# VectorE's program in source order, a 64-column chunk loop and the first projection ahead of the second, in a hybrid RWKV-7 and Conformer step

## The chip, the cores and the metric

The kernel runs on one core of one Trainium2 chip. The metric is device microseconds of one execution. The engines are TensorE (PE in the profile, its weight loads PEld), VectorE (DVE), ScalarE (ACT), GpSimd (POOL), and SyncE (SP), which issues most DMAs.

## The reference, cut to what matters

One layer for 512 prompt tokens and 8 single-token samples, all in float32; the kernel lays them side by side as 520 columns.

```
xn = _rmsnorm(x, norm_g);  proj = xn @ w_in              # 2048 -> 11392
r, k, v, xw, xa = xs[...]                                # token-shifted columns of proj
decay = exp(-exp(w_log(xw)));  a = sigmoid(a0 + xa @ a_lora_b)
for t:                                                   # per head, S is 64 x 64
    sa = S @ a_t;  S = S * w_t + sa b_t^T + v_t k_t^T;  o_t = S @ r_t
o   = groupnorm(o) + bonus
y_a = (o * silu(gate_a)) @ w_proj_a                      # the first projection
u   = glu(proj);  c = depthwise_conv31(u) + conv_b
y_b = (silu(layernorm(c)) * silu(gate_b)) @ w_proj_b     # the second projection
m   = sigmoid(ga) * y_a + sigmoid(gb) * y_b
h   = x + m @ w_out
h   = h + sigmoid(h @ w_ple_gate) * (p @ w_ple)
y   = _rmsnorm(h) * final_g
```

## The kernel before

Activations lie channel-major, 128 channels by 520 tokens a tile. Every large product goes through `gemm` and `step` (L153 to L175): a step is one 128 x 128 weight tile times 520 columns. Activation and weight are each split in a high part (`wh`, `xh`, `hi`) and a low part (`wl`, `xl`, `lo`), and three of the four products are summed, in two column halves of 260, so a step is six matmuls; there are 2224 steps. `prepare` (L117) makes `wh` on ScalarE and `wl` on VectorE for four steps at a time (a half of a loaded block). It runs two halves ahead of use (`AHEAD`) in four buffers (`WB`). Weights arrive in 512 KB DMAs on SyncE's queue.

The first 16 k-steps make four output tiles at once. Then a loop over eight pairs of heads p runs nine gemms of 16 steps each: k, r, v, gate_a, the two halves of the GLU input, gate_b and two merge gates (`merge`, L652, which stores its sigmoid to DRAM, `sga_d` and `sgb_d`). 16 more merge gates follow, then the two projections (L846), `w_out` (L856), and the gated embedding with the final norm (`gate`, `finish`).

All small work is written as generators that `tick` advances after each step; `yield n` means n steps later. So the numbers behind `yield` set where PE's small matmuls stand between the steps, since PE's order is that of the source (`manual_schedule`, L54). The order on VectorE, ScalarE, GpSimd and SyncE is left to the tile framework's scheduler.

The generators:
- `wkv(p)` (L358): the recurrence of two heads in eight chunks of 64 tokens. It makes decays and keys, the 128 x 128 products within chunks (L446), a triangular inverse in 31 dependent pairs of VectorE instructions (`tm`, `ti`, L480), and then the **chunk loop** (L546). Each turn has three links, `ly` steps apart: `x = ar @ suv` for both heads (L549, with `oc` of the chunk before at L551); `x = ttb @ xs` (L556), whose copy to `suv` is made by VectorE for one head (L557) and ScalarE for the other (L558), with a GpSimd copy `xu` (L561); and the state update `bkt @ suv` (L564), after which VectorE makes the next chunk's `suv` (L568) and the state `sf` (L571). A group norm follows, and 16 64 x 64 transposes (L595, L596).
- `conv(i)` (L621): the depthwise convolution, 30 dependent VectorE instructions `c` (L643).
- `samples` and `lnorm` (L678, L715): the recurrence of the eight samples, and the layer norm of the convolution.
- `finish(h)` (L904): the final norm of token half h, which scales the 16 tiles `h2` by `rf` on VectorE or GpSimd (`ON_POOL`) and stores them in `GROUPS`.

Of the kernel before, what the change touches and what calls it, by code (L numbers as in the profile page):

```python
# [17 lines left out]
P = 128  # L18
# [12 lines left out]
WB, AHEAD, LAST, WARM = 4, 2, 12, 14  # L31
# [6 lines left out]
GROUPS = ([range(4 * _g, 4 * _g + 4) for _g in range(4)],  # L38
          [range(0, 1), range(12, 13), range(1, 4), range(4, 8), range(13, 16), range(8, 12)])
ON_POOL = ((1, 2, 3, 5, 6, 7, 9, 10, 11, 13, 14, 15), (12, 13, 14, 15))  # L40
# [8 lines left out]
TILES += [M_SA + _i for _i in range(16, 32)]  # L49


def body(nc, tc, a):
    with ExitStack() as es:
# [21 lines left out]
        vec, act, gps = nc.vector, nc.scalar.activation, nc.gpsimd  # L75
# [14 lines left out]
        for j in range(KD):  # L90
            seq += [a["wpa"][j], a["wpb"][j]]
# [42 lines left out]

        stream = prepares()
# [115 lines left out]
        def colsum(lhsT, hi, lo, n):  # L251
# [3 lines left out]
            for h in range(0, n, step):  # L255
                o = aux()
                nc.tensor.matmul(o[:, :step], lhsT=lhsT, rhs=hi[:, h:h + step], start=True, stop=False)
                nc.tensor.matmul(o[:, :step], lhsT=lhsT, rhs=lo[:, h:h + step], start=False, stop=True)
# [34 lines left out]
        for i, n, o in ((0, 252, first[3][0]), (252, 252, first[3][1]), (504, 16, first[2][0])):  # L293
            o = o[:, HF:HF + n]
            nc.tensor.matmul(o, lhsT=sums[:, 2, :], rhs=sqs[0][:, i:i + n], start=True, stop=True)
# [3 lines left out]
        sxs.close()  # L299

# [7 lines left out]
        def parts(x, n=T):  # L308
            hi = gp.tile([P, T], F32R, name="hi", tag="g")[:, :n]
            lo = gp.tile([P, T], F32R, name="lo", tag="g")[:, :n]  # L310
            split(x, hi, lo)
# [15 lines left out]
        def shifted(m, o, out):  # L327
# [6 lines left out]
            vec.scalar_tensor_tensor(out, p, omu[:, m:m + 1], q, op0=ALU.mult, op1=ALU.add)  # L334
# [6 lines left out]

        tw = et("tw")
        shifted(M_L, o_lora, tw)
        act(tw[0:64, :], tw[0:64, :], AF.Tanh)
        for i, x in enumerate(parts(tw)):
            for j in range(2):
                act(tw2[half(i), j, :], x[half(j), :].bitcast(F32), AF.Copy)
# [8 lines left out]
        flag = {"inv": None, "done": -1, "loop": -1, "conv": 0, "yp": None}  # L356

        def wkv(p, k, box):  # L358
# [3 lines left out]
            dma(out=lor, in_=a["lora"][:, :, p * P:(p + 1) * P])  # L362
            kk = gt("kk")
# [3 lines left out]
            sh, sl_ = parts(sq)  # L367

            yield 16 if p == 0 else 5
            lorh = kq.tile([P, 2, P], F32R, name="lorh")  # L370
            lorl = kq.tile([P, 2, P], F32R, name="lorl")
            split(lor, lorh, lorl)
            yield 7
            sg = gt("sig")
            av = gt("a")
            for j, (out, off) in enumerate(((sg, O_W0), (av, O_A0))):
                for h in range(2):
                    hs = slice(h * HF, (h + 1) * HF)
                    o = aux()
                    nc.tensor.matmul(o[:, :HF], lhsT=lorh[:, j, :], rhs=tw2[:, j, hs], start=True, stop=False)  # L380
                    nc.tensor.matmul(o[:, :HF], lhsT=lorl[:, j, :], rhs=tw2[:, j, hs], start=False, stop=True)
                    act(out[:, hs], o[:, :HF], AF.Sigmoid, bias=col(off, p))
                yield 2
# [3 lines left out]
            yield 2  # L387
# [33 lines left out]
            yield 8  # L421
# [6 lines left out]
            for h in range(2):  # L428
                s = half(h)
                tt(vec, ar[h][s, :, h, :], ch(kk)[s], ep[s, :, 0:64], ALU.mult)  # L430
                tt(gps, ar[h][s, :, 1 - h, :], ch(r)[s], ep[s, :, 1:65], ALU.mult)
                tt(vec, bk[s, :, h, :], ch(b)[s], ch(em)[s], ALU.mult)
# [4 lines left out]
            yield 9  # L437
# [4 lines left out]
            for c0 in (0, 4):  # L442
                os = [aux().rearrange("p (c x) -> p c x", x=P) for _ in range(2)]
                for c in range(4):
                    for h in range(2):
                        nc.tensor.matmul(os[h][:, c, :], lhsT=bk[half(h), c0 + c].rearrange("p a t -> p (a t)"),  # L446
                                         rhs=ar[h][half(h), c0 + c].rearrange("p a t -> p (a t)"), start=True, stop=True)
                for h in range(2):
# [4 lines left out]
                    tt(vec, nbr[s, c0:c0 + 4, i:i + 64], o[s, :, i:i + 64], mk(s, 64, 64), ALU.mult)  # L453
                    tt(vec, f2(ar[h][u, c0:c0 + 4]), o[u], mk(u, 64 * h, P), ALU.mult)
                    yield 2
# [8 lines left out]
            nc.tensor.transpose(o[:48, :P], sp.rearrange("p a b -> p (a b)"), ident)  # L464
# [10 lines left out]
            yield 5  # L475
# [3 lines left out]
            yield 5  # L479
# [521 lines left out]
```

## Time and profile before

| what | value |
|---|---|
| time, median of 3 runs | 1880.88 us (1878.25 to 1882.21) |
| time of the profiled execution | 1881.83 us |
| its span, first to last instruction | 1880.0 us |
| VectorE, the weights' low parts `wl` (L78) | 386.8 us, 541 times |
| VectorE, the convolution `c` (L643) | 188.9 us, 240 times |
| VectorE, `tm` and `ti` of the inverse | 106.5 us and 72.8 us |
| GpSimd, the copies `xu` (L561) | 51.4 us, 128 times |

A row of the costliest groups or of the windows gives busy time and count of instructions. Matmuls overlap, so what a matmul costs is read from the start of one to the start of the next, in the timeline; its own duration is longer. A timeline row merges equal neighbours: start, length, engine, line, what is written from what, the count, and idle time before it with what ended it. A row of the waits gives who waited for whom: total us, number of waits, the longest. PEclk is the granted TensorE clock as a share of full speed.

### The profile page before, as it was taken

To read this page: it belongs to the slowest core of one execution; us is meant where nothing else is said; L and a number is where in the kernel's file an instruction comes from. 1 tells how busy PE (TensorE), PEld (TensorE's weight loads), DVE (VectorE), ACT (ScalarE), POOL (GpSimd) and SP (SyncE) were. 2 spreads that over 40 slices of the span, in tenths; PEclk is the share of its full clock that TensorE was granted. 3 is DMA by queue.
4 is the path that set the end of the run, shared out by engine and by line. 5 is a ranking of instruction groups with operands and counts; after the bars stand their busy time and mean duration, and the time that the engine had idled before them with its cause. 6 is when DMAs were issued, how large, how long until landed. Compare 5 with 4: busy or idle time off the path is not lost.

```text
span 1880.0 us, 37810 instructions
## 1 busy us (share of the span) xinstructions
PE 1823.0 (97%) x15352; PEld 1782.9 (95%) x15352; DVE 1276.0 (68%) x2337; ACT 771.7 (41%) x1478; POOL 397.7 (21%) x514
## 2 busy tenths in 40 slices
PE   9999999999999999999999999999999999999995
PEld 8998998999999999999999999999999999999995
DVE  6679897697797877977977885495433333334457
ACT  6734335336345354363363332464222222243343
POOL 1212214123213213222231372030111000011103
PEclk9999998999999999999999999999999999999998
DMA  7242332432332323323323343456444433252232
GB/s 229 81 117 72 103 100 69 94 106 81 101 102 83 99 88 98 101 86 88 112 76 94 124 153 120 146 165 201 136 136 136 136 118 96 90 192 95 95 103 91
DMA packets 116367, 211.97 MB, mean 113 GB/s; under 512 B 47312, under 2 KB 55632, under 8 KB 116192
## 3 DMA queue, kind: packets, MB, share of 16 engines
q1 hardware_dynamic: 114592, 207.95, 35.9%
q8 instruction: 120, 1.97, 0.4%
q10 hardware_dynamic: 1600, 1.60, 0.3%
q14 instruction: 55, 0.45, 0.1%
HBM read 184.43 MB, written 25.08 MB: 111 GB/s over the span
## 4 chain that ended last, share of the span: by engine, by line
PE 69%; DVE 19%; issue 4%; ACT 3%; POOL 3%; DMA 1%; SPq 0%; DVEq 0%; POOLq 0%; ACTq 0%
PE mm L165 62%; DVE tm L78 5%; DVE wl L78 4%; DVE ti L484 3%; DVE c L643 2%; PE aux L596 1%; PE aux L165 1%; PE aux L446 1%; PE aux L549 1%; ACT wh L81 1%; DVE p L78 1%; PE aux L595 1%; POOL ar L78 1%; PE aux L564 1%; DVE sq L394 1%
## 5 line engine op out<-in xcount | busy, mean ns | idle before, releaser
L165 PE MATMUL mm<-xh,wh 128*128 128x260 f32 x2784 | 593.3, 295 | 0.9 <-ACT xh L219 0.5
L81 ACT ACTIVATE wh<-w 128x512 fp32r<-128x512 f32 (+1 forms) x541 | 338.5, 627 | 621.0 <-PE mm L165 532.2
L78 DVE TENSOR_TENSOR wl<-w,wh 128x512 fp32r<-128x512 f32 (+1 forms) x541 | 386.8, 717 | 280.3 <-ACT wh L81 276.5
L165 PE MATMUL mm<-xh,wl 128*128 128x260 f32 x2784 | 569.4, 286 | 4.8 <-DVE wl L78 4.8
L165 PE MATMUL mm<-xl,wh 128*128 128x260 f32 x2784 | 568.9, 286 | 0.3 <-DVE xl L220 0.3
L165 PEld LDWEIGHTS mm<-xh,wh 128*128 128x128 f32 x2784 | 437.0, 193 | 9.4 <-ACT wh L81 1.1
L165 PEld LDWEIGHTS mm<-xh,wl 128*128 128x128 f32 x2784 | 436.5, 192 | 5.5 <-DVE wl L78 5.4
L165 PEld LDWEIGHTS mm<-xl,wh 128*128 128x128 f32 x2784 | 437.2, 192 | 0.6 <-DVE xl L220 0.5
L165 PE MATMUL mm<-hi,wl 128*128 128x260 f32 x1600 | 333.4, 283 | 3.1 <-DVE wl L78 3.1
L165 PE MATMUL mm<-hi,wh 128*128 128x260 f32 x1600 | 333.3, 283 | 0.0
L165 PE MATMUL mm<-lo,wh 128*128 128x260 f32 x1600 | 332.6, 283 | 0.0
L165 PEld LDWEIGHTS mm<-hi,wl 128*128 128x128 f32 x1600 | 251.0, 189 | 3.3 <-DVE wl L78 3.3
L165 PEld LDWEIGHTS mm<-hi,wh 128*128 128x128 f32 x1600 | 252.1, 189 | 0.1
L165 PEld LDWEIGHTS mm<-lo,wh 128*128 128x128 f32 x1600 | 251.9, 189 | 0.0
L643 DVE SCALAR_TENSOR_TENSOR c<-u,prm,c 128x482 f32<-128x482 f32 (+14 forms) x240 | 188.9, 787 | 3.8
L561 POOL COPY xu<-suv 64x64 f32<-64x64 f32 x128 | 51.4, 402 | 280.8 <-DVE suv L557 271.6
L78 DVE TENSOR_TENSOR tm<-ti,ni 128x16 f32<-128x16 f32 (+30 forms) x248 | 106.5, 429 | 6.0
L78 POOL TENSOR_TENSOR sq<-hi,lo 128x520 f32<-128x520 f32 (+1 forms) x20 | 24.4, 1224 | 337.5 <-DVE one L875 184.0
L78 DVE TENSOR_TENSOR p<-mm,rs 128x520 f32<-128x520 f32 x78 | 54.1, 693 | 48.0 <-PE mm L165 47.8
L484 DVE TENSOR_REDUCE ti<-tm 128x8 f32<-128x16 f32 (+30 forms) x248 | 72.8, 293 | 6.1
L573 ACT ACTIVATE o<-aux 64x64 f32<-64x64 f32 x128 | 28.0, 219 | 92.2 <-DVE sf L571 91.3
L78 POOL TENSOR_TENSOR s<-s,s 128x520 f32<-128x520 f32 x16 | 25.4, 1587 | 171.7 <-DVE s L78 138.8
(243 smaller groups left out, 1774.3 us busy)
## 6 DMA issues: line engine op xcount, KB each, us to landing
w<-in_win SPq DMA_DIRECT2D x170, 512.0 KB, 3.8
w<-in_wout SPq DMA_DIRECT2D x32, 512.0 KB, 3.8
w<-in_wpg SPq DMA_DIRECT2D x24, 512.0 KB, 3.6
w<-in_wpa SPq DMA_DIRECT2D x16, 512.0 KB, 3.6
w<-in_wpb SPq DMA_DIRECT2D x16, 512.0 KB, 3.7
wx<-in_wpg SPq DMA_DIRECT2D x32, 256.0 KB, 4.1
x<-in_xT SPq DMA_DIRECT2D x16, 260.5 KB, 6.8
sga_d<-p SPq DMA_DIRECT2D x16, 260.0 KB, 2.3
```

Of the source, the lines that this page charges most:

```text
L78: eng.tensor_tensor(out, x, y, op=op)
L81: behind.append(act(hi, x, AF.Copy))
L165: nc.tensor.matmul(o[h], lhsT=w[:, used[0] % 4, :], rhs=x[:, h * HF:(h + 1) * HF], start=(k == 0 and i == 0), stop=(k == nk - 1 and i == 2))
L394: vec.reciprocal(rn[:, h:h + 130], rn[:, h:h + 130])
L446: nc.tensor.matmul(os[h][:, c, :], lhsT=bk[half(h), c0 + c].rearrange("p a t -> p (a t)"), rhs=ar[h][half(h), c0 + c].rearrange("p a t -> ...
L484: last = vec.tensor_reduce(ti[:, :, t], tm[:, :, :t + 1], axis=AX.X, op=ALU.add)
L549: nc.tensor.matmul(x[:, h, :], lhsT=ar[h][:, c].rearrange("p a t -> p (a t)"), rhs=suv[:, h, c, :], start=True, stop=True)
L561: gps.tensor_copy(xu[half(h)], suv[half(h), h, c, :])
L564: nc.tensor.matmul(x[half(h), 3, :], lhsT=bkt[:, c, h * 64:h * 64 + 64], rhs=suv[:, h, c, :], start=True, stop=True)
L573: act(o1[half(1 - h), c, :], x[half(1 - h), h, :], AF.Copy)
L595: nc.tensor.transpose(ot[a0, c, :], o1[a1, c, :], ident[a1, a1])
L643: vec.scalar_tensor_tensor(c[:, d:NPR], u[:, 0:NPR - d], cw[:, k:k + 1], c[:, d:NPR], op0=ALU.mult, op1=ALU.add)
```

## The change

1. **VectorE's order.** From the end of the first 16 k-steps up to the end of the first projection, `manual_schedule` holds VectorE too, so that it runs in the order of the source. The calls on `vec`, `gps` and the small matmuls go through `Paced`, which adds a modelled duration to a clock; `yield ROOM` lets a generator go on only when VectorE's modelled clock is at most `LAG` (1 us) ahead of TensorE's. The inverse, the convolution, the group norm, the samples and the layer norm are cut up with such yields. Generators get a priority (`start(g, first)`). A weight half's `wl` is written one half later than its `wh` (`lower`), and `AHEAD` is 3.
2. **The chunk loop.** L549 and L551 become 64-column matmuls, one for each head and result, and `oc` is summed in PSUM. The copies `xu` and `o1` go; `xs` is one ScalarE copy; both `suv` copies are ScalarE's. The normalised result is written to `on` so that four 128 x 128 transposes stand for the 16 small matmuls with eight 64 x 64 transposes. For p = 7 `ly` is 5, not 7.
3. **The first projection** runs for all 16 tiles before the second begins; the result times the gate goes back to `sga_d` and is loaded again. The last part of `lnorm` runs beside it.
4. **The end.** `finish(0)` works in eight groups of two tiles, later, with 4 of its 16 products on GpSimd, not 12.

```diff
-WB, AHEAD, LAST, WARM = 4, 2, 12, 14
+WB, AHEAD, LAST, WARM = 4, 3, 12, 14
-ON_POOL = ((1, 2, 3, 5, 6, 7, 9, 10, 11, 13, 14, 15), (12, 13, 14, 15))
+ON_POOL = ((1, 5, 9, 13), (12, 13, 14, 15))
...
+        def work(us):
+            clock["dve"] = max(clock["dve"], clock["pe"]) + us
+        vec = Paced(nc.vector, lambda name, n: work(0.0069 * n if name == "reciprocal" else 0.14 + 0.00107 * n))
+        gps = Paced(nc.gpsimd, lambda name, n: work(0.0007 * n if n > 64 else 0.05))
...
                 if e[0] > 0:
                     e[0] -= 1
                     continue
+                if e[2] and clock["dve"] > clock["pe"] + LAG:
+                    continue
...
+        order.enter_context(tc.manual_schedule(engines={mybir.EngineType.DVE}))
...
             for c in range(NCH):
                 x = aux().rearrange("p (c x) -> p c x", x=64)
                 for h in range(2):
-                    nc.tensor.matmul(x[:, h, :], lhsT=ar[h][:, c].rearrange("p a t -> p (a t)"), rhs=suv[:, h, c, :], start=True, stop=True)
-                if c:
-                    nc.tensor.matmul(oc[:, c - 1, :], lhsT=nbr[:, c - 1, :], rhs=xu, start=True, stop=True)
+                    pe.matmul(x[half(h), 0, :], lhsT=ar[h][:, c, h, :], rhs=suv[:, h, c, :], start=True, stop=True)
+                for h in range(2):
+                    pe.matmul(oc[half(h), c, :], lhsT=ar[h][:, c, 1 - h, :], rhs=suv[:, h, c, :], start=True, stop=False)
...
-                vec.tensor_copy(suv[0:64, 0, c, :], x[0:64, 2, :])
-                act(suv[64:128, 1, c, :], x[64:128, 2, :], AF.Copy)
-                xu = kq.tile([P, 64], F32, name="xu", bufs=2)
                 for h in range(2):
-                    gps.tensor_copy(xu[half(h)], suv[half(h), h, c, :])
+                    act(suv[half(h), h, c, :], x[half(h), 2, :], AF.Copy)
                 yield ly
...
+                for h in range(2):
+                    pe.matmul(oc[half(h), c, :], lhsT=nbr[:, c, h * 64:h * 64 + 64], rhs=suv[:, h, c, :], start=False, stop=True)
...
+        for j in range(KD):
+            s1 = gt("s1")
+            dma(out=s1, in_=sga_d[j])
+            tt(vec, v2(s1), gemm(8, ya), v2(s1), ALU.mult)
+            dma(out=sga_d[j], in_=s1)
         drain()
+        order.close()
```

How rows move. On TensorE, in one turn of the chunk loop, the first link before (`ar` holds one head's products, `mm` rows are steps):

```order
L165 MATMUL mm<-xh,wl 128x260 x2
L549 MATMUL aux<-suv,ar_2546 128x64
L549 MATMUL aux<-suv,ar_2547 128x64
L551 MATMUL oc<-xu,nbr_798 128x64
L165 MATMUL mm<-xh,wh 128x260 x2
```

and now (L67 is the wrapper's line, L211 the step's):

```order
L211 MATMUL mm<-xh,wl 128x260 x2
L67 MATMUL aux<-suv,ar_5873 64x64
L67 MATMUL aux<-suv,ar_5874 64x64
L67 MATMUL oc<-suv,ar_5873 64x64
L67 MATMUL oc<-suv,ar_5874 64x64
L211 MATMUL mm<-xh,wh 128x260 x2
```

Three results of 128 rows became four of 64 rows. The last link, before two calls of 64 rows (`L564 MATMUL aux<-suv,bkt 64x64 x2`), is now

```order
L211 MATMUL mm<-xl,wh 128x260 x2
L211 MATMUL mm<-xh,wl 128x260 x2
L67 MATMUL aux<-suv,bkt 64x64 x2
L67 MATMUL oc<-suv,nbr_787 64x64 x2
L211 MATMUL mm<-xh,wh 128x260 x2
```

so that `oc` of the chunk is finished in the same link, with two calls more.

On VectorE, beside the chunk loop, between the weights' rows `wl`, before:

```order
L78 TENSOR_TENSOR wl<-w,wh 128x512 x3
L78 TENSOR_TENSOR p<-mm,rs 128x520
L557 COPY suv<-aux 64x64
L334 SCALAR_TENSOR_TENSOR r<-p,omu,q 128x520
L386 SCALAR_TENSOR_TENSOR cs<-cst,sig 128x256 x2
L391 TENSOR_SCALAR sq<-aux 128x260 x2
L568 SCALAR_TENSOR_TENSOR suv<-sf,epl,aux 64x64 x2
L571 SCALAR_TENSOR_TENSOR sf<-sf,epl,aux 128x64
L78 TENSOR_TENSOR wl<-w,wh 128x512 x2
```

and the same place now:

```order
L67 TENSOR_TENSOR wl<-w,wh 128x512
L67 RECIPROCAL sq<-sq 128x130 x3
L67 TENSOR_TENSOR p<-mm,rs 128x520
L67 TENSOR_TENSOR wl<-w,wh 128x512
L67 SCALAR_TENSOR_TENSOR suv<-sf,epl,aux 64x64 x2
L67 SCALAR_TENSOR_TENSOR sf<-sf,epl,aux 128x64
L67 RECIPROCAL sq<-sq 128x130
L67 TENSOR_TENSOR wl<-w,wh 128x512
```

The copy `suv<-aux` is gone, and a `wl` stands after every four other instructions, where before three `wl` stood together with ten others behind them.

At the end, VectorE around the scaling of the first token half (`h` by `rf`; `wx` are the last weights), before:

```order
L911 RECIPROCAL rf<-rf 128x260
L78 TENSOR_TENSOR wl<-wx,wh 128x512
L78 TENSOR_TENSOR h_20216<-h_20216,rf 128x260
L78 TENSOR_TENSOR h_20217<-h_20217,rf 128x260
L78 TENSOR_TENSOR h_20218<-h_20218,rf 128x260
L78 TENSOR_TENSOR s<-s,h_20219 128x260
L78 TENSOR_TENSOR h_20219<-h_20219,rf 128x260
L78 TENSOR_TENSOR h_20219<-s,sq 128x260
L78 TENSOR_TENSOR wl<-wx,wh 128x512
```

and now:

```order
L67 TENSOR_TENSOR h_20011<-h_20011,rf 128x260 x2
L67 TENSOR_TENSOR wl<-wx,wh 128x512
L67 TENSOR_TENSOR acc<-acc,sq 128x260
L67 TENSOR_TENSOR h_20012<-h_20012,rf 128x260
L67 TENSOR_TENSOR wl<-wx,wh 128x512
L67 TENSOR_TENSOR h_20012<-h_20012,rf 128x260 x2
L67 TENSOR_TENSOR wl<-wx,wh 128x512
```

Twelve products instead of four are VectorE's, one to three of them between two `wl`.

More of the change, by code (lines that the diff above doesn't have):

```diff
@@ L333, in shifted, with last @@
             gps.tensor_copy(q[:, NPR:T], muss[:, m, :])
-            vec.scalar_tensor_tensor(out, p, omu[:, m:m + 1], q, op0=ALU.mult, op1=ALU.add)
+            def last():
+                yield 4
+                vec.scalar_tensor_tensor(out, p, omu[:, m:m + 1], q, op0=ALU.mult, op1=ALU.add)
+                box[name] = out
+            start(last(), first=True)
         def silu(o, out):
@@ L340, in silu, with lowrank @@
             tt(gps, out, p, s, ALU.mult)
[L342 to L347, printed above, removed]
+        def lowrank():
+            while "tw" not in flag:
+                yield 1
+            tw = flag["tw"]
+            act(tw[0:64, :], tw[0:64, :], AF.Tanh)
+            yield 3
+            for i, x in enumerate((yield from parts(tw))):
+                for j in range(2):
+                    act(tw2[half(i), j, :], x[half(j), :].bitcast(F32), AF.Copy)
+            flag["low"] = True
         tts = kq.tile([P, NCH, 64], F32, name="tts")
@@ L571, in wkv @@
                 vec.scalar_tensor_tensor(sf, s0, epl[:, c:c + 1], x[:, 3, :], op0=ALU.mult, op1=ALU.add)
-                for h in range(2):
-                    act(o1[half(1 - h), c, :], x[half(1 - h), h, :], AF.Copy)
                 yield ly
-            nc.tensor.matmul(oc[:, NCH - 1, :], lhsT=nbr[:, NCH - 1, :], rhs=xu, start=True, stop=True)
             flag["done"] = p
@@ L604, in gnorm @@
         def gnorm(o, og, n):
-            oh, ol = parts(o, n)
+            oh, ol = yield from parts(o, n)
             yield 3
@@ L610, in gnorm @@
             act(sq, oc[:, :n], AF.Square)
-            sh, sl = parts(sq, n)
+            yield 2
+            sh, sl = yield from parts(sq, n)
             yield 4
@@ L740, in lnorm @@
                 else:
+                    yield ROOM
                     tt(vec, vs, vs, sq, ALU.add)
-            vh, vl = parts(vs)
+            yield 1
+            vh, vl = yield from parts(vs)
             yield 4
@@ L746, in lnorm @@
                 act(rl[:, h:h + n], o[:, :n], AF.Sqrt, scale=1.0 / 1024, bias=eps[:, 1:2])
-            vec.reciprocal(rl, rl)
-            yield 7
+            yield 5
+            for h in range(0, T, 130):
+                vec.reciprocal(rl[:, h:h + 130], rl[:, h:h + 130])
+                yield ROOM
+            while not flag["merged"]:
+                yield 1
             prev = None
```

344 lines of the change are left out of this document (216 added, 128 removed).

## The prediction

> **What bounds the kernel now.** I read the page first: engine shares, then the chain of work that ended last.
>
> ```profile
> PE 1823.0 (97%) x15352; PEld 1782.9 (95%) x15352; DVE 1276.0 (68%) x2337; ACT 771.7 (41%) x1478; POOL 397.7 (21%) x514
> PE 69%; DVE 19%; issue 4%; ACT 3%; POOL 3%; DMA 1%; SPq 0%; DVEq 0%; POOLq 0%; ACTq 0%
> ```
>
> TensorE is busy for 97%, yet only 69% of the chain is its own: busy does not mean at its rate. So the next view is busy time by stage, for all work and then for the steps' matmuls (L165) alone. The columns are the stretch, its length, busy time and count of PE, PEld, DVE, ACT and POOL, the granted clock, DMA share and GB/s.
>
> ```profile
> 54.60:1280.70 1226.10, 1190.78 (x10142) 1154.63 (x10143) 984.54 (x1905) 540.05 (x1089) 325.48 (x447) 0.97 0.35 103
> 1280.70:1833.70 553.00, 553.00 (x4610) 552.90 (x4609) 225.13 (x333) 179.13 (x298) 46.77 (x33) 1.00 0.39 126
> 1833.70:1880.00 46.30, 27.34 (x202) 25.87 (x200) 32.30 (x45) 18.60 (x34) 18.35 (x19) 0.80 0.27 93
> ```
>
> ```profile
> 54.60:1280.70 1226.10, 1071.87 (x8161) 0.97 0.35 103
> 1280.70:1833.70 553.00, 553.00 (x4610) 1.00 0.39 126
> ```
>
> From 1280.7 us on TensorE runs nothing but steps: 553.00 us / 4610 = 0.120 us a matmul. At that rate the 8161 matmuls of the middle stage take 979 us of its 1226. The other 247 us are: idle, 1226.1 - 1190.8 = **35.3 us**; lost clock, (1 - 0.97) x 1226 = **37 us** (31 to 43, as the 0.97 is rounded); and the rest, **175 us**, the 1981 small matmuls of recurrence, norms and transposes. The change can win in these three and at the end. Who ended the idle time says the view of the waits, TensorE's alone, for the middle stage (total us, times, longest):
>
> ```profile
> PE aux L564 <- ACT suv L558: 10.4, 10, 3.7
> PE aux L549 <- DVE suv L568: 7.6, 8, 3.5
> PE mm L165 <- DVE wl L78: 4.4, 2, 3.1
> PE aux L595 <- DVE o L78: 4.1, 5, 1.0
> PE aux L515 <- ACT yt L503: 2.0, 2, 1.8
> PE aux L257 <- ACT hi L81: 1.9, 1, 1.9
> PE aux L258 <- DVE lo L78: 1.8, 1, 1.8
> ```
>
> These are 29 waits of mostly about 1 us. The timeline of TensorE shows what such a wait costs besides:
>
> ```profile
> 660.15 0.40 PE L165 MATMUL mm<-xl,wh 128*128 128x260 f32 x2
> 660.39 0.40 PE L165 MATMUL mm<-xh,wl 128*128 128x260 f32 x2
> 661.48 0.24 PE L595 MATMUL aux<-cst,o 64*64 64x64 f32 x1 [0.69 <-DVE o L78]
> 661.91 0.24 PE L595 MATMUL aux<-cst,o 64*64 64x64 f32 x1
> 666.53 0.64 PE L165 MATMUL mm<-xh,wl 128*128 128x260 f32 x2
> 666.97 0.64 PE L165 MATMUL mm<-xh,wh 128*128 128x260 f32 x2
> ```
>
> Pairs of matmuls start 0.24 us apart before the idle 0.69 us, and 0.44 us apart some 5 us behind it: half rate for some microseconds. That is where the 37 us of clock go: 37 / 29 = 1.3 us a wait, more than the wait itself.
>
> [...]
>
> Why does the longest of them wait? The timeline of VectorE at one such place, and from the view of line 557 who waited for its copy:
>
> ```profile
> 643.03 1.17 DVE L78 TENSOR_TENSOR tm<-ti,ni 128x224 f32<-128x224 f32 x1
> 644.24 0.39 DVE L484 TENSOR_REDUCE ti<-tm 128x8 f32<-128x224 f32 x1
> 645.13 0.21 DVE L557 COPY suv<-aux 64x64 f32<-64x64 f32 x1
> ```
>
> ```profile
>   ACT suv L558: 96.1, 40
> ```
>
> A 0.21 us copy stands in VectorE's queue behind the inverse of the next pair, and ScalarE's half of `suv`, on which TensorE's L564 waits, comes after it. VectorE is not full: 985 of 1226 us. Its order makes the waits.
>
> **The change, part by part.** *Small matmuls.* The rows of the two groups in one turn of the chunk loop, and of four 128 x 128 transposes:
>
> ```profile
> 607.83 0.56 PE L549 MATMUL aux<-suv,ar 128*128 128x64 f32 x4
> 608.23 0.39 PE L551 MATMUL oc<-xu,nbr 128*128 128x64 f32 x2
> 608.42 0.49 PE L165 MATMUL mm<-xh,wh 128*128 128x260 f32 x2
> 608.75 0.40 PE L165 MATMUL mm<-xl,wh 128*128 128x260 f32 x2
> ```
>
> ```profile
> 604.15 0.40 PE L165 MATMUL mm<-xh,wl 128*128 128x260 f32 x2
> 604.48 0.34 PE L564 MATMUL aux<-suv,bkt 128*64 128x64 f32 x4
> 604.74 0.50 PE L165 MATMUL mm<-xh,wh 128*128 128x260 f32 x2
> 605.08 0.40 PE L165 MATMUL mm<-xl,wh 128*128 128x260 f32 x2
> ```
>
> ```profile
> 686.04 0.60 PE L526 MATMUL aux<-cst,v 128*128 128x128 f32 x4
> 686.39 0.48 PE L165 MATMUL mm<-xh,wh 128*128 128x260 f32 x2
> 686.71 0.40 PE L165 MATMUL mm<-xl,wh 128*128 128x260 f32 x2
> ```
>
> What a group costs is the time from its start to the second pair behind it, less that pair's 0.24 us, and what the pair ahead took over 0.24. L549 with L551: 608.75 - 607.83 - 0.24 = 0.68 us. L564: 605.08 - 604.48 - 0.24 + 0.09 = 0.45 us. Both new groups have L564's form with twice the calls. Its four matmuls take 0.26 us up to the next pair; four more add about 0.2 (as a link of two calls has its own start and drain already in the 0.45). So the first link goes from 0.68 to 0.66, the last from 0.45 to 0.66: +0.19 us a turn, 64 turns: +12. Turn 0 had no L551 (0.2 us a p, +2), and the last L551 group of each p, L575, goes (about 0.2 us, -2). If the two heads' 64-column matmuls did not overlap in the new form, four more would cost what L549's four do (608.23 - 607.83 = 0.4 us), 0.2 us a group more, 128 groups: +26 on top. At best the new groups cost no more than the old, 12 less. The norm's transposes start 0.43 us apart a chunk (661.48 to 661.91), 8 x 0.43 + 0.2 = 3.6 us a p; in their place stand four of L526's form, 686.71 - 686.04 - 0.24 = 0.43 us: 8 x 3.2 = -25. Sum of small matmuls: **-13 us** (-25 to +13).
>
> [...] The first link now pays that 0.09 us, which the 0.45 contains.
>
> *Waits.* L564's go with VectorE's copy: both copies are ScalarE's, behind one TensorE link and with 2.9 us until the next (four steps of 0.72); 9 of 10.4 us. L595's: the norm's result now has steps between each of its parts; 3 of 4.1. L257 and L258 (one place, p = 0): a step stands between high part, low part and sum; 3.7. Late `wl`: one of two, 2.2. That is 17.9 of 35.3 us, **-18**. L549's 7.6 us stay: its `suv` is still VectorE's. The bounds are 0 and -35.
>
> *Clock.* It goes with the number of waits: 9 of 10, 4 of 5, 2 and 1 are 16 of 29, times 37: **-20 us** (0 to -37).
>
> *The end.* GpSimd's 12 products run for 11.8 us, and beside them VectorE is slowed:
>
> ```profile
> 1841.33 11.81 POOL L78 TENSOR_TENSOR h<-h,rf 128x260 f32<-128x260 f32 x12 [15.01 <-DVE rf L911]
> ```
>
> ```profile
> 1837.61 0.69 DVE L78 TENSOR_TENSOR wl<-wx,wh 128x512 fp32r<-128x512 f32 x1 [0.95 <-ACT wh L81]
> 1846.99 1.22 DVE L78 TENSOR_TENSOR wl<-wx,wh 128x512 fp32r<-128x512 f32 x1
> ```
>
> The `wl` at 1846.99 is the one behind VectorE's run of `h`; TensorE waits 3.1 us for a `wl` there, and the clock is 0.80 in this stage. With 4 products on GpSimd, and VectorE's twelve between the `wl`, I take the wait and some of the clock away: **-5 us** (-8 to +4, if the eight products more, each as long as the `wl` of 0.69 us, hold up the `wl` behind them).
>
> *At nothing.* The first projection's 16 stores and loads of 0.27 MB add 8.5 MB in 128 steps (92 us), 92 GB/s on top of weights at 91 (0.52 MB in eight steps). A stretch with more than that left TensorE full:
>
> ```profile
> 1269.00:1316.00 47.00, 47.00 (x394) 47.00 (x393) 24.43 (x39) 18.87 (x33) 4.56 (x3) 1.00 0.62 201
> ```
>
> The gain of that edit is that the last of the layer norm gets 92 us of cover; it was covered already, since the stage behind 1280.7 has no gap. Without that cover each of the 16 tiles would wait for 0.27 MB at 201 GB/s, 1.3 us, 21 in all.
>
> *An added wait.* Each VectorE instruction now holds back all behind it, `wl` among them. A `wl` is written two halves, 8 x 0.72 = 5.8 us, ahead of use, so a hold-up of up to 5 us is hidden from the steps; a chunk's `suv` has only 2.9 us.
>
> **Sum.** -13 - 18 - 20 - 5 = -56 us. The profiled execution took 1881.8 us (span 1880.0 and 1.8 around it), 0.9 above the median of the runs; 1881 - 56 = **1825 us**.
>
> **Rivals.**
>
> (B) Nearly all waits go, L549's too: idle -33, clock -34, small matmuls -13, end -5: 1796. For it: VectorE has 241 us free in the stage. Against: `suv` still stands behind other rows of VectorE.
>
> (C) The wait moves. L564's 9 us and their 10/29 of the clock, 13 us, come back as waits for `suv` on VectorE (L549), since the inverse and the convolution are still paced into the same stretch: 1825 + 22 = 1847. For it: the existing L549 waits, 8 of them.
>
> (D) Slower: VectorE's written order is wrong by more than its slack. The place is the first half of each chunk loop, where the next pair's preparation stands between the `suv`. One late `suv` costs 1 us and 1.3 us of clock. From 56 / 2.3 = 24 of them, three a p, the gain is gone; five a p are 8 x 5 x 2.3 = 92 us: 1917. For it: a queue that cannot pass a waiting head, and the pace itself, which counts a convolution tap as 0.14 + 0.00107 x 497 = 0.67 us where the group's row has 0.787; 30 taps are 3.5 us a p that the pace does not see, more than a link's 2.9.
>
> ```profile
> L643 DVE SCALAR_TENSOR_TENSOR c<-u,prm,c 128x482 f32<-128x482 f32 (+14 forms) x240 | 188.9, 787 | 3.8
> ```
>
> Against: the 241 us of free VectorE time.
>
> (E) The waits go, but the half-rate stretches have another cause and stay: -13 - 18 - 5 = -36, 1845. Against: the half rate at 666 us right behind the wait. [...]
>
> (F) C and half of D's price cancel the rest: no change.
>
> Chances: forecast 0.45, B 0.2, C 0.2, E 0.02, F 0.05, D 0.08. About 0.2% is what a measurement of this kernel can tell from no change. Faster 0.87, same 0.05, slower 0.08. The forecast's own range is 1806 to 1845; the 8-in-10 range takes in C with its spread, E and most of B: 1790 to 1866.
>
> **What would show it.** L564 gone from TensorE's waits; a granted clock of 0.98 or 0.99 in the middle stage; the new transposes below half a microsecond a p; GpSimd with 4 products at the end and no wait for `wl` there. Wrong if L549 or `wl` lead the waits with over 20 us (C, D), or if the groups of 64-column matmuls take over 0.9 us.

## The result, and the profile after

The changed kernel takes **1836.68 us** (median of 4 runs, 1833.2 to 1838.8) against 1880.85 for the kernel before: ratio 0.9762, 95% interval 0.9744 to 0.9780. The forecast was 1825, the range 1790 to 1866: right in direction and within the range, 12 us too low.

The page of the changed kernel, engine shares and the chain that ended last:

```profile
PE 1785.5 (97%) x15576; PEld 1744.7 (95%) x15576; DVE 1279.5 (70%) x2300; ACT 743.3 (41%) x1355; POOL 353.3 (19%) x370
...
PE 74%; DVE 19%; issue 3%; ACT 1%; POOL 1%; DMA 1%; SPq 0%; DVEq 0%; ACTq 0%; POOLq 0%
```

Its windows, cut at the same steps as before (stretch, length, busy time and count of PE, PEld, DVE, ACT, POOL, granted clock, DMA share, GB/s): the middle stage, then projections with `w_out` and gates, then the end.

```profile
53.50:1237.00 1183.50, 1153.73 (x10368) 1116.37 (x10367) 978.81 (x1839) 496.46 (x943) 276.54 (x302) 0.99 0.36 107
1237.00:1790.10 553.10, 553.10 (x4611) 552.99 (x4610) 236.83 (x353) 194.50 (x321) 58.84 (x41) 1.00 0.44 142
1790.10:1835.10 45.00, 27.05 (x202) 25.59 (x200) 30.75 (x52) 18.62 (x34) 9.96 (x11) 0.81 0.28 96
```

Read against the rows of before: the middle stage went from 1226.1 to 1183.5 us, the stage of pure steps stayed at 553.1, the end went from 46.3 to 45.0. Nearly the whole gain is in the middle (42.6 of the 44.9 us by which the span got shorter). There, idle TensorE fell only from 35.3 to 1183.5 - 1153.7 = 29.8 us. Half-rate time, by the trace's clock records, fell from 61 to 34 us, which is 31 and 17 us lost. The other 23 us or so of the gain are shorter small matmuls. The waits changed their names:

```profile
PE aux L67 <- DVE d L67: 8.9, 11, 2.2
PE aux L67 <- ACT suv L644: 5.5, 2, 3.0
PE mm L211 <- DVE wl L67: 4.6, 3, 2.0
PE aux L67 <- ACT xs L640: 4.1, 3, 1.9
PE aux L67 <- DVE suv L67: 3.4, 2, 1.8
PE aux L67 <- ACT yt L591: 2.5, 3, 2.2
```

The columns are who waited for whom, total us, number of waits, the longest. The first is new: `d` is VectorE's transpose of the inverse's result (d11), and TensorE did not wait for it before. The second is the state link's (L564 before), two waits in place of ten. So the forecast's total is nearly met by other terms than the forecast's. That is what the experiments had to sort out.

### The profile page after: what moved, and what is told of

Same layout as the page of the kernel before. It is cut to its first block, busy times and chain, and to the rows that moved or that the text cites. A ratio compares the mean times of both kernels' runs of the same rounds, so it can differ in the third digit from the quotient of the medians.

```text
span 1835.1 us, 37880 instructions
## 1 busy us (share of the span) xinstructions
PE 1785.5 (97%) x15576; PEld 1744.7 (95%) x15576; DVE 1279.5 (70%) x2300; ACT 743.3 (41%) x1355; POOL 353.3 (19%) x370
## 4 chain that ended last, share of the span: by engine, by line
PE 74%; DVE 19%; issue 3%; ACT 1%; POOL 1%; DMA 1%; SPq 0%; DVEq 0%; ACTq 0%; POOLq 0%
PE mm L211 68%; PE aux L67 5%; DVE wl L67 4%; DVE tm L67 4%; DVE c L67 3%; DVE ti L67 2%; PE aux L211 1%; DVE p L67 1%; DVE sq L67 1%; DVE on L67 1%; PE oc L67 1%; DMA w<-in_win 0%; DVE h L67 0%; DVE suv L67 0%; DVE m L67 0%
## 5 line engine op out<-in xcount | busy, mean ns | idle before, releaser
L211 PE MATMUL mm<-xh,wh 128*128 128x260 f32 x2784 | 589.1, 293 | 0.4 <-ACT xh L266 0.4
L211 PE MATMUL mm<-xh,wl 128*128 128x260 f32 x2784 | 565.9, 285 | 4.6 <-DVE wl L67 4.6
L211 PE MATMUL mm<-xl,wh 128*128 128x260 f32 x2784 | 566.0, 285 | 0.3 <-DVE xl L67 0.3
L67 DVE TENSOR_TENSOR wl<-w,wh 128x512 fp32r<-128x512 f32 (+1 forms) x541 | 397.5, 738 | 200.4 <-ACT wh L154 198.3
L211 PEld LDWEIGHTS mm<-xh,wh 128*128 128x128 f32 x2784 | 432.6, 191 | 12.1 <-ACT wh L154 0.6
L211 PEld LDWEIGHTS mm<-xh,wl 128*128 128x128 f32 x2784 | 433.7, 191 | 5.2 <-DVE wl L67 5.2
L211 PEld LDWEIGHTS mm<-xl,wh 128*128 128x128 f32 x2784 | 433.8, 191 | 0.6 <-DVE xl L67 0.5
L211 PE MATMUL mm<-hi,wl 128*128 128x260 f32 x1600 | 333.5, 284 | 2.6 <-DVE wl L67 2.6
L211 PE MATMUL mm<-hi,wh 128*128 128x260 f32 x1600 | 333.3, 283 | 0.0
L211 PE MATMUL mm<-lo,wh 128*128 128x260 f32 x1600 | 332.4, 282 | 0.0
L211 PEld LDWEIGHTS mm<-hi,wl 128*128 128x128 f32 x1600 | 250.7, 189 | 3.1 <-DVE wl L67 3.1
L211 PEld LDWEIGHTS mm<-hi,wh 128*128 128x128 f32 x1600 | 252.0, 189 | 0.1
L211 PEld LDWEIGHTS mm<-lo,wh 128*128 128x128 f32 x1600 | 251.8, 189 | 0.0
L67 DVE SCALAR_TENSOR_TENSOR c<-u,prm,c 128x482 f32<-128x482 f32 (+14 forms) x240 | 201.6, 840 | 4.4
L67 DVE TENSOR_TENSOR tm<-ti,ni 128x16 f32<-128x16 f32 (+30 forms) x248 | 104.1, 420 | 4.9
L67 POOL TENSOR_TENSOR sq<-hi,lo 128x520 f32<-128x520 f32 (+1 forms) x20 | 24.3, 1220 | 337.8 <-DVE one L67 184.0
L67 DVE TENSOR_TENSOR p<-mm,rs 128x520 f32<-128x520 f32 x78 | 53.7, 689 | 48.3 <-PE mm L211 48.2
L67 DVE TENSOR_REDUCE ti<-tm 128x8 f32<-128x16 f32 (+30 forms) x248 | 73.6, 297 | 8.5
L67 DVE TENSOR_TENSOR s<-mm,s 128x520 f32<-128x520 f32 x32 | 22.4, 700 | 65.9 <-PE mm L211 65.9
L67 POOL COPY nsh<-p 128x9 f32<-128x9 f32 x25 | 14.9, 597 | 238.0 <-DVE p L67 238.0
L67 DVE SCALAR_TENSOR_TENSOR suv<-sf,epl,aux 64x64 f32<-64x64 f32 x112 | 31.1, 278 | 38.4 <-PE aux L67 22.4
```

The lines of the kernel that those rows point to most:

```text
L67: return f(*args, **kw)
L211: nc.tensor.matmul(o[h], lhsT=w[:, used[0] % 4, :], rhs=x[:, h * HF:(h + 1) * HF], start=(k == 0 and i == 0), stop=(k == nk - 1 and i == 2))
```

## The experiments

Three theories. **Theory 1** is the prediction's: a fixed VectorE order takes waits away, and clock with them. **Theory 2**: the gain is in the small matmuls, half-rate stretches follow something else than waits, and VectorE runs late because the load model prices work too low. **Theory 3** came up on the way. Each run's ratio is to runs of the kernel before on the same chip.

### The parts apart

*VectorE's order given back to the scheduler:*

```diff
-        order.enter_context(tc.manual_schedule(engines={mybir.EngineType.DVE}))
```

> The changed kernel with VectorE's order given back to the scheduler; the source, its pauses and the 64-column loop stay. Theory 1 (the order takes the waits away, as the prediction has it): idle of TensorE in the middle stage comes back from 29.8 us to 48 or more and some clock with it, 1855 to 1875 us. Theory 2 (the gain is in the small matmuls, the order gives about as much as it takes): within 8 us of the changed kernel, 1829 to 1845 us.

Measured: 1921.0 us, ratio 1.0213 (1.0196 to 1.0230): 84 us slower than the changed kernel and slower than before. Theory 1 had the sign, neither the size. Its waits, first row, and VectorE's timeline at one such wait (TensorE stands idle from 409.4 on):

```profile
PE aux L67 <- DVE d L67: 67.9, 12, 12.5
```

```profile
409.51 0.41 DVE L67 TENSOR_TENSOR on<-o,m 64x256 f32<-64x256 f32 x1
409.84 0.57 DVE L67 TENSOR_TENSOR tm<-ti,ni 128x248 f32<-128x248 f32 x1
...
412.87 0.42 DVE L67 TENSOR_REDUCE ti<-tm 128x8 f32<-128x256 f32 x1
...
419.10 0.90 DVE L67 STREAM_TRANSPOSE d<-tts 32x256 f32<-32x256 f32 x2 [3.40 <-DMA tts<-td]
```

The scheduler lets the last pairs of the inverse (`tm`, `ti`) stand among the norm's rows; the inverse ends at 413.3, its round trip through DRAM lasts until 419.1, and TensorE has long been there. The source's pauses were written for the other order. So this run prices the pair, not the order alone.

*The 64-column loop and its transposes alone, in the kernel before:* part 2 of the change, L549 to L596, with the new pauses of the norm but without the shorter `ly` of p = 7 (one of the edits shown).

```diff
-                    nc.tensor.matmul(x[:, h, :], lhsT=ar[h][:, c].rearrange("p a t -> p (a t)"), rhs=suv[:, h, c, :], start=True, stop=True)
+                    nc.tensor.matmul(x[half(h), 0, :], lhsT=ar[h][:, c, h, :], rhs=suv[:, h, c, :], start=True, stop=True)
```

> The kernel before with the 64-column chunk loop and the norm's four 128 x 128 transposes alone; VectorE's order, the projections and the end are those of before. Theory 2 (small matmuls: about 24 us less, read from the trace of after; the half-rate stretches that came at the norm's 64 x 64 transposes go too, up to 14 us): 1843 to 1857 us. Theory 1 (small matmuls -13 as predicted, the waits stay, save those on the copies to suv): 1861 to 1870 us.

Measured: 1879.6 us, ratio 0.9986 (0.9976 to 0.9997): almost nothing. Both theories missed. The windows tell where it went; first three p of the steady loop, then the last p with samples, layer norm and the first projections, before:

```profile
580.60:972.40 391.80, 384.58 (x3331) 371.87 (x3327) 319.55 (x651) 173.38 (x360) 99.27 (x154) 0.98 0.32 94
972.40:1303.70 331.30, 321.55 (x2659) 314.23 (x2656) 243.56 (x411) 132.57 (x269) 98.90 (x97) 0.96 0.45 141
```

and with the loop alone:

```profile
578.30:961.20 382.90, 371.49 (x3415) 357.77 (x3411) 318.46 (x632) 164.56 (x318) 79.49 (x102) 1.00 0.33 96
961.20:1302.30 341.10, 319.75 (x2702) 310.38 (x2699) 244.83 (x402) 125.52 (x241) 89.12 (x65) 0.96 0.44 137
```

The loop wins 8.9 us in three p and loses 9.8 behind them, where idle goes from 9.8 to 21.4 us. In the three p its shorter small matmuls and the clock save 13.1 us of busy time, and 4.2 us of that come back as idle time. Most of the new waits are for the loop's and the norm's own operands (in the whole execution):

```profile
PE aux L596 <- DVE on L78: 16.7, 6, 3.3
PE aux L548 <- DVE suv L565: 12.2, 8, 4.0
```

Behind the three p, waits for `suv` and `on` make 14 of the 21 us.

*The reverse: the loop and norm of before in the changed kernel:*

```diff
-                    pe.matmul(x[half(h), 0, :], lhsT=ar[h][:, c, h, :], rhs=suv[:, h, c, :], start=True, stop=True)
+                    pe.matmul(x[:, h, :], lhsT=ar[h][:, c].rearrange("p a t -> p (a t)"), rhs=suv[:, h, c, :], start=True, stop=True)
...
-                    act(suv[half(h), h, c, :], x[half(h), 2, :], AF.Copy)
+                vec.tensor_copy(suv[0:64, 0, c, :], x[0:64, 2, :])
+                act(suv[64:128, 1, c, :], x[64:128, 2, :], AF.Copy)
```

> The changed kernel with the chunk loop and the norm's 64 x 64 transposes of before, one copy to suv on VectorE again, written between the pauses of the change (VectorE's order, the projections and the end are those of the change). If parts add up, this is the changed kernel plus the 1.3 us that the chunk loop won alone: 1838 us. Theory 2 (small matmuls cost 24 us more, 16 of them plain time, the rest half-rate stretches behind the 64 x 64 groups; the copies to suv wait behind taps in the fixed order): 1861 to 1875 us.

Measured: 1835.8 us, ratio 0.9761 (0.9745 to 0.9778): the same as the changed kernel. Theory 2's 1861 falls. (Only the shorter `ly` of p = 7 stays from part 2.) Its middle stage and its leading wait there:

```profile
53.70:1236.70 1183.00, 1172.51 (x10138) 1141.79 (x10138) 971.16 (x1882) 522.65 (x1060) 335.50 (x438) 0.99 0.34 106
```

```profile
PE aux L67 <- ACT suv L646: 9.5, 4, 2.6
```

The same 1183 us, made up otherwise: idle 10.5 us, not 29.8, and 19 us more of busy TensorE; half-rate time is 34 us in both. So the whole gain in time comes without the new loop; at this point the loop adds nothing to it. This gave theory 3: **the order takes 25 of the 35 us of waiting away; the 64-column loop saves some 20 us of matmuls, and in the changed kernel they came back as waits on a late VectorE.**

*The end of before, and the first projection beside the second, as before:*

```diff
-ON_POOL = ((1, 5, 9, 13), (12, 13, 14, 15))
+ON_POOL = ((1, 2, 3, 5, 6, 7, 9, 10, 11, 13, 14, 15), (12, 13, 14, 15))
```

> The changed kernel with the end of before: 12 products on GpSimd, stores of four tiles, pauses of 3 and 8 steps. Predicted term: 5 us slower, 1842 us. Theory from the trace of after, whose end is only 1.2 us shorter and still waits 2.4 us for a wl: 1837 to 1839 us.

Measured: 1834.9 us, ratio 0.9760 (0.9740 to 0.9780): no difference. The changed kernel (first row) still waits for a `wl` at the end, 2.4 us where the old end (second row) waits 3.1:

```profile
1803.79 0.39 PE L211 MATMUL mm<-hi,wl 128*128 128x260 f32 x1 [2.39 <-DVE wl L67]
```

```profile
PE mm L211 <- DVE wl L67: 3.1, 1, 3.1
```

```diff
-        for j in range(KD):
-            s1 = gt("s1")
-            dma(out=s1, in_=sga_d[j])
-            tt(vec, v2(s1), gemm(8, ya), v2(s1), ALU.mult)
-            dma(out=sga_d[j], in_=s1)
...
+            tt(vec, v2(s1), gemm(8, ya), v2(s1), ALU.mult)
             tt(vec, v2(s2), gemm(8, yb), v2(s2), ALU.mult)
```

> The changed kernel with the first projection made tile by tile together with the second, as before. Predicted (that edit at nothing, the layer norm is covered without it): 1835 to 1839 us. Rival (the 16 us that the last part of the middle stage got shorter come from that cover): 1847 to 1855 us, with an idle TensorE ahead of the projections.

Measured: 1856.5 us, ratio 0.9867 (0.9852 to 0.9881): 20 us slower. The rival wins, by the row of the first 32 projection steps, and by the wait in that stretch:

```profile
1238.10:1279.60 41.50, 31.49 (x194) 28.79 (x193) 31.07 (x36) 20.74 (x34) 14.72 (x9) 0.75 0.47 160
```

```profile
PE mm L212 <- DVE lo L67: 8.2, 7, 1.9
```

32 steps are 23 us; here 41.5, with 10 us idle and a clock of 0.75: 18.5 of the 20. In the kernel before, the layer norm's last `lo` starts about 1 us behind the first projection step (1281.9 and 1280.7 us); in this run it starts 25 us behind it (1263.6 and 1238.1). In the new order the layer norm ends later, and needs the first projection as its cover.

### What halves the clock

*Waits without small matmuls:* behind each of the 16 tiles of the output projection TensorE waits for four copies, then runs one matmul.

```diff
+            z = st("z")
+            act(z[:, 0:64], o[:, 0, :64], AF.Copy)
+            for i in range(3):
+                act(z[:, 64 * i + 64:64 * i + 128], z[:, 64 * i:64 * i + 64], AF.Copy)
+            nc.tensor.matmul(aux()[:, :64], lhsT=ident, rhs=z[:, 192:256], start=True, stop=True)
```

> The changed kernel; behind each of the 16 tiles of the output projection TensorE waits for a chain of four small copies on ScalarE that begins with that tile's result, and then runs one 64-column matmul that nothing uses: an idle TensorE of about 1.2 us, 16 times, with 11.5 us of steps between. Prediction's mechanism (each wait costs 1.3 us of clock besides): 16 x 2.5 = 40, 1877 us, granted clock 0.9 in that stage. Rival (one idle microsecond among full work costs no clock): 16 x 1.2 = 20, 1857 us, clock 1.00.

*Small matmuls without a wait:*

```diff
+            for c in range(NCH):
+                nc.tensor.transpose(ot[a0, c, :], ident[a1, a0], ident[a1, a1])
+                nc.tensor.matmul(ot[a1, c, :], lhsT=ident[a0, a0], rhs=ident[a0, a0], start=True, stop=True)
```

> The changed kernel; behind each of the 16 tiles of the output projection TensorE runs eight 64 x 64 transposes and eight 64 x 64 matmuls on the constant identity, which wait for nothing and are used by nothing. By the old norm's rows a group takes 3.5 us: 16 x 3.5 = 56, 1893 us if small matmuls leave the clock alone (the prediction's mechanism: clock is lost behind waits). If such a group counts as little activity and halves the clock for 3.4 to 6.8 us: 1.7 to 3.4 us more each, 1920 to 1948 us, and a granted clock of 0.90 to 0.95 in that stage.

Measured: 1869.4 us for the waits (ratio 0.9933, 0.9910 to 0.9956), 1915.1 for the small matmuls (1.0178, 1.0160 to 1.0197). The window of the 256 steps and the waits in it, with the waits:

```profile
1423.10:1638.30 215.20, 191.85 (x1570) 188.57 (x1568) 66.39 (x98) 65.23 (x145) 1.55 (x1) 1.00 0.31 98
```

```profile
PE aux L994 <- ACT z L993: 23.3, 16, 1.5
```

and the window and one group with the small matmuls:

```profile
1420.80:1681.00 260.20, 260.20 (x1923) 240.69 (x1921) 67.28 (x100) 51.69 (x82) 2.65 (x2) 0.92 0.25 78
```

```profile
1432.04 0.40 PE L211 MATMUL mm<-hi,wl 128*128 128x260 f32 x2
1432.37 0.24 PE L993 MATMUL aux<-cst 64*64 64x64 f32 x1
...
1435.55 0.46 PE L994 MATMUL aux<-cst 64*64 64x64 f32 x2
1435.93 0.80 PE L211 MATMUL mm<-hi,wh 128*128 128x260 f32 x2
1436.53 0.64 PE L211 MATMUL mm<-lo,wh 128*128 128x260 f32 x2
1436.96 0.64 PE L211 MATMUL mm<-hi,wl 128*128 128x260 f32 x2
```

Sixteen waits of 1.46 us leave the clock at 1.00. The total lies between the two forecasts: the 256 steps take 184.2 us in the changed kernel, so each place costs 31 / 16 = 1.9 us, 1.46 of it idle and the rest the added matmul and the steps' start behind it. Sixteen groups that wait for nothing, 3.6 us each, bring the clock to 0.92: the clock records hold 13 stretches of 3.41 us at half rate, each beginning within 1 us of a group's end (here the steps' pairs start 0.43 us apart from 1436.5 on). The total is 5 us below the range for halved clocks; three groups left no stretch. The prediction's 1.3 us of clock for each wait does not hold: 16 waits cost no clock here, and 13 of 16 groups of 64 x 64 matmuls with no idle time in them had 3.41 us at half rate behind them. (Half of the group are transposes; no run parts them from the plain matmuls.)

That does not clear all waits. The half-rate stretches of a run all begin on one grid of 3.413 us (in the clock records of the kernel before and of the changed one they last 3.413 or 6.827 us, save the last, and one period of 3.4133 us fits all their starts to within 0.02 us), so the traces can be read window by window. In the 14 traces, from 60 us on, a full-rate window that held only steps and up to 1.83 us of idle time never halved the clock of the next one, and a window with 1.95 us or more of idle time always did; in between both occur. (In the traces of the two kernels these two limits are 1.76 us, in the window at 436.0 us of the changed kernel, and 2.01 us, in the one at 1134.8 us of the kernel before.) A single wait of 1.46 us stays below that. In the changed kernel (a window of the grid and the stretch behind it; columns as above):

```profile
562.30:565.72 3.42, 1.14 (x10) 0.93 (x8) 3.42 (x3) 0.33 (x1) 2.43 (x2) 1.00 0.25 65
565.72:572.55 6.83, 6.13 (x33) 5.79 (x34) 6.64 (x11) 3.82 (x7) 2.23 (x3) 0.50 0.12 44
```

All seven stretches of its middle stage stand behind windows with 1.4 to 2.3 us of idle time, small matmuls beside it where it is under 1.9 us. Of the 13 in the kernel before, seven stand behind a group of 64 x 64 matmuls with at most 0.7 us of idle time in the window (34 us at half rate), and six behind 1.8 to 3.0 us of idle time (27 us). So in these traces a wait had no price in clock of its own; what counted was how much of one window was left without steps.

### Why VectorE is late

VectorE's and GpSimd's timelines of the changed kernel ahead of one wait for `d`:

```profile
776.18 2.35 DVE L67 SCALAR_TENSOR_TENSOR c<-u,prm,c 128x483 f32<-128x483 f32 x3
...
779.05 4.42 DVE L67 SCALAR_TENSOR_TENSOR c<-u,prm,c 128x486 f32<-128x486 f32 x3
...
786.00 1.10 DVE L67 TENSOR_TENSOR wl<-w,wh 128x512 fp32r<-128x512 f32 x1
...
787.70 0.89 DVE L67 STREAM_TRANSPOSE d<-tts 32x256 f32<-32x256 f32 x2
```

```profile
778.63 1.64 POOL L67 TENSOR_TENSOR og<-og,bv 128x512 f32<-128x512 f32 x1 [0.62 <-ACT og L689]
...
780.36 1.60 POOL L67 TENSOR_TENSOR og<-og,sl 128x512 f32<-128x512 f32 x1
781.93 1.03 POOL L67 TENSOR_SCALAR ttb<-tts 64x512 f32<-64x512 f32 x1
...
785.46 1.11 POOL L67 TENSOR_SCALAR ttb<-tts 64x512 f32<-64x512 f32 x1
```

Three taps (instructions of the convolution) take 2.35 us, then three beside two products and a `ttb` of GpSimd 4.42. Over the whole trace a tap takes 0.73 us with no GpSimd instruction beside it (154 taps) and 1.70 us where one of GpSimd's products runs beside at least nine tenths of it (16 taps). The load model adds 0.0007 x 512 = 0.36 us to VectorE's clock for such a GpSimd instruction; an estimate from these rows of what it costs VectorE is (4.42 - 2.35) / 3 = 0.7 us. (Its own duration, 1.0 to 1.6 us, is not what that clock should be charged.)

*A truer price for GpSimd:*

```diff
-        gps = Paced(nc.gpsimd, lambda name, n: work(0.0007 * n if n > 64 else 0.05))
+        gps = Paced(nc.gpsimd, lambda name, n: work(0.0010 * n if n > 64 else 0.05))
```

> The changed kernel with the load model's price of a GpSimd operation at 0.0010 us an element instead of 0.0007; it only changes when VectorE's next piece is let go. Theory 2 (the model prices work too low, so VectorE is late): waits for d and wl shorter, 1827 to 1834 us. Rival (work put off piles up ahead of the next convolution or chunk): 1838 us or more.

Measured: 1820.0 us, ratio 0.9667 (0.9652 to 0.9682), 17 less than the changed kernel. Middle stage:

```profile
53.40:1220.20 1166.80, 1146.17 (x10368) 1109.21 (x10367) 968.34 (x1835) 496.07 (x942) 276.29 (x302) 0.99 0.36 108
```

Idle 20.6 us (from 29.8), half-rate time 17 us (from 34): 9 and 8 us. The total goes theory 2's way and 7 us beyond its range, though the waits for `d` stay (9.1 us); the others shrank.

*A higher price still:*

```diff
-        gps = Paced(nc.gpsimd, lambda name, n: work(0.0007 * n if n > 64 else 0.05))
+        gps = Paced(nc.gpsimd, lambda name, n: work(0.0014 * n if n > 64 else 0.05))
```

> The changed kernel with a GpSimd price of 0.0014 us an element (0.73 us for 520; the rows have 1.2 to 1.7). If a truer price is better throughout: 1815 us or less. If the gain of 0.0010 is used up and work put off piles up ahead of the next convolution: 1822 us or more.

Measured: 1816.4 us (1815.7 to 1817.3), ratio 0.9661 (0.9647 to 0.9676): the fastest kernel of this study, 20 below the changed one, though not clearly apart from the price of 0.0010. It lies between the two forecasts, so neither is borne out: idle time fell to 17.3 us, half-rate time went up again to 27.

```profile
53.20:1217.60 1164.40, 1147.10 (x10363) 1111.79 (x10362) 973.31 (x1835) 494.63 (x940) 277.22 (x302) 0.99 0.36 108
```

*Two attempts on the wait for* `d` *that failed:* the transposes four steps earlier,

```diff
-            yield 16
+            yield 12
             for h in range(2):
                 vec.transpose(d11[h * 64:h * 64 + 32], tts[h * 64:h * 64 + 32, :, 0:32])
-            yield 4
+            yield 8
```

> The changed kernel with the transposes of tts to d11 standing four steps (2.9 us) earlier in VectorE's order; the matmuls that read d11 stay at their step. Theory 2 (VectorE runs late behind convolution taps that GpSimd's products slow down, and d is what TensorE then waits for): the waits for d fall from 8.9 us to under 3 and one or two half-rate stretches with them, 1822 to 1831 us. Rival (the round trip of the inverse's result through DRAM is late): VectorE itself waits at d11, TensorE waits as long as before, 1836 us or more.

and, at a price of 0.0010, the edges of `q` on ScalarE:

```diff
-            gps.memset(q[:, 0:1], 0.0)
-            gps.tensor_copy(q[:, NPR:T], muss[:, m, :])
+            act(q[:, 0:1], p[:, 0:1], AF.Copy, scale=0.0)
+            act(q[:, NPR:T], muss[:, m, :], AF.Copy)
```

> The kernel with the GpSimd price of 0.0010, and the two small edges of the shifted tile q written by ScalarE in place of GpSimd, where they stand behind two products of 1.3 and 1.6 us while VectorE's next row (k) waits 1.3 us for them and d stands behind it. If that hold-up makes the 1.9 us wait for d in the steady p: waits for d under 4 us in all (9.1 in that kernel), 1808 to 1815 us. If the wait has another cause: 1818 to 1822 us.

Measured: 1840.4 (ratio 0.9778, 0.9763 to 0.9793) and 1819.3 us (0.9675, 0.9654 to 0.9696). In the first the waits for `d` went, as theory 2 said, and others took their place:

```profile
PE mm L211 <- DVE wl L67: 10.2, 6, 3.3
PE aux L67 <- ACT yt L591: 8.8, 5, 4.2
```

In the second they went from 9.1 to 7.4 us and the time did not move. So it is not these rows' places: while VectorE is late, moving one row passed the wait on in the first run and won nothing in the second.

*The old loop at the higher price:*

```diff
-                    pe.matmul(x[half(h), 0, :], lhsT=ar[h][:, c, h, :], rhs=suv[:, h, c, :], start=True, stop=True)
+                    pe.matmul(x[:, h, :], lhsT=ar[h][:, c].rearrange("p a t -> p (a t)"), rhs=suv[:, h, c, :], start=True, stop=True)
...
-        gps = Paced(nc.gpsimd, lambda name, n: work(0.0007 * n if n > 64 else 0.05))
+        gps = Paced(nc.gpsimd, lambda name, n: work(0.0014 * n if n > 64 else 0.05))
```

> The kernel with the old chunk loop in the new order, and a GpSimd price of 0.0014. Theory 3 (the 64-column loop saves TensorE about 24 us, but in the changed kernel VectorE's lateness gave them back; with the old loop in this order little idle time is left, 10.5 us, for a price to take away): 1830 to 1840 us, so that at this price the loop is worth some 20 us. Rival (the price is worth its 20 us whatever the loop, and the loop is worth nothing): 1812 to 1820 us.

Measured: 1837.2 us, ratio 0.9759 (0.9740 to 0.9779). The totals are theory 3's: the price is worth nothing with the old loop (1835.8 without) and 20 us with the new one; the loop is worth nothing at the low price and 1837.2 - 1816.4 = 21 us at the higher (18 by the ratios, as the two runs had different chips).

```profile
53.30:1228.80 1175.50, 1171.55 (x10140) 1140.28 (x10139) 945.85 (x1867) 518.44 (x1051) 333.08 (x438) 0.99 0.35 105
1228.80:1787.90 559.10, 555.48 (x4603) 554.67 (x4602) 249.71 (x372) 201.31 (x332) 58.44 (x41) 0.99 0.45 145
```

Here the loop's price can be read: busy TensorE in the middle stage 1171.6 against 1147.1 us, 24 more (some 2 of them half rate). But idle is 4 us against 17, so the new loop still gives 13 us back as waits and keeps only 1175.5 - 1164.4 = 11 us in its own stage. Another 6 us of the difference lie behind the stage (559.1, not 553), where with the old loop the projections wait for `lo`; there the old loop loses most of the 1183.0 - 1175.5 = 7.5 us that the price wins it in the middle stage. So theory 3 holds for the matmul time saved and its return as waits; that the higher price sets all of it free is not shown.

## Why the prediction came out, point by point

| term | predicted | shown |
|---|---|---|
| small matmuls | -13 | about -23 (19 of it the loop and its transposes, given back as waits) |
| waits | -18 | -25 by the order with the old loop; -5.5 in the changed kernel |
| clock | -20 | -14: 17 less behind 64 x 64 groups, 3 more behind waits |
| the end | -5 | about 0 |
| first projection | 0 | 0 against before; without it +20 |
| sum | -56 | -44 |

- **Small matmuls**: right in mechanism, mis-sized. By the prediction's own method the new link costs 596.27 - 595.55 - 0.24 + 0.09 = 0.57 us, where the forecast had 0.66; 0.09 us in 128 links are 11.5 us, about the missing 10. The four matmul rows added to a link cost 0.12 us (0.48 against 0.36 for L564's four), not 0.2. The transposes, 0.43 us by forecast, take 776.72 - 776.04 - 0.24 = 0.44.

```profile
595.55 0.34 PE L67 MATMUL aux<-suv,ar 128*64 128x64 f32 x4
595.71 0.29 PE L67 MATMUL oc<-suv,ar 128*64 128x64 f32 x4
595.93 0.51 PE L211 MATMUL mm<-xh,wh 128*128 128x260 f32 x2
596.27 0.41 PE L211 MATMUL mm<-xl,wh 128*128 128x260 f32 x2
```

```profile
776.04 0.60 PE L67 MATMUL aux<-cst,on 128*128 128x128 f32 x4
776.39 0.49 PE L211 MATMUL mm<-xh,wh 128*128 128x260 f32 x2
776.72 0.40 PE L211 MATMUL mm<-xl,wh 128*128 128x260 f32 x2
```

- **Waits**: the old wait on the state link (L564, for ScalarE's `suv`) fell from ten waits with 10.4 us to two with 5.5, where the forecast left one of 1.4. The step that failed is that the other waits stay or go as listed: waits for `d` came (8.9 us) and those for `xs` grew from 1.8 to 4.1 us, those for `wl` stayed (4.4 and 4.6) where one was to go, and those for VectorE's `suv`, which were to stay at 7.6, fell to 3.4. Rival C's mechanism, a wait that moves, took hold, though not at the place it named. Its ground, taps that the pace prices too low, was in the prediction's rival D; the runs tested GpSimd's price, which the prediction did not look at. No run raised the price of the taps or changed `LAG`, which might do the same.
- **Clock**: the size was near (the 37 us were 31 by the records), the step "1.3 us a wait" wrong. It read a cause from one place (666 us) where a wait of 0.69 us and 3.6 us of 64 x 64 matmuls stood together, and gave the clock to the wait. Rival E, "another cause", was right for the seven stretches behind such groups, 17 us of lost clock, which went with the transposes of part 2 and not with the waits. The other six stood behind long waits; there clock does go with waits, and in the changed kernel the new waits lose 17 us where the old ones lost 14. E's consequence, that the stretches stay, did not come: they fell from 61 to 34 us in the fixed order even with the 64 x 64 groups kept (20 us of the 34 behind such groups).
- **The end**: the wait for `wl` was to go with 8 of GpSimd's products; it shrank from 3.1 to 2.4 us.
- **First projection**: "it was covered already" held for the kernel before only. The cover was judged in the old order, and the change itself moves the layer norm later.

The changed kernel's own column is -23, -5.5, -14 and -1. That the forecast came within 12 us is in part luck: a term too small (the matmuls) nearly made up for terms too large (the waits, the clock with its wrong cause, the end). By the run with the old loop, the gain in time is that of the order, with the first projection ahead as its cover.

Open: why the new loop leaves VectorE later than the old one at the same price was not tried. VectorE has about the same work in a shorter p (978.8 and 971.2 us in the middle stage, 24 us less of TensorE to hide it), which would do it, but that is argued.

## What to carry to other kernels

Time saved on the bounding engine counts only as far as the next engine in its program keeps up: measure the saving with that engine's lateness reduced (here by a price in a load model, which brought out 11 us in the loop's own stage) before calling an edit worthless. A pace that decides an in-order queue should charge what the neighbour engine's work costs that queue (here some 0.7 us an instruction by the estimate above, where the model had 0.36). And an edit's cover is judged in the order that the change makes, not in the one it replaces.

## What the runs showed of the hardware that was not expected

- 3.6 us of uninterrupted 64 x 64 matmuls halved the clock for 3.41 us in 13 of 16 cases (0.92 over the 260.2 us), while 16 idle gaps of 1.46 us among full steps did so never (1.00 over the 215.2 us). In the changed kernel a gap of 2.56 us at 437.7 us had no half-rate stretch behind it: it fell on two windows of the grid, 1.76 and 0.80 us. One of 1.42 us at 1068.1 had one: it fell in one window, together with eight small matmuls.
- In the 14 traces a full-rate window of 3.413 us with 1.95 us or more of idle time always halved the clock of the next one; up to 1.83 us beside steps alone never did (2.01 and 1.76 us in the traces of the two kernels).
- A tap of VectorE took 0.73 us alone (154 taps) and 1.70 us beside GpSimd's products (16 taps).
- Four more rows of 64-column matmuls in a group that already has four cost 0.12 us (0.48 against 0.36 for the group), a third of the first four's 0.36.
